# Who waits for GpSimd's two output stores: ScalarE in place of SyncE, in a mixture-of-experts MLP

## The chip, the cores and the metric

The kernel runs on one core of a Trainium2 chip. The metric is the device time of one execution in microseconds (us), the median of several runs. Beside it there is one profiled execution, whose trace is read below.

## The reference

Eight experts, each a two-layer perceptron on its own 256 tokens, in float32:

```python
n_experts, capacity, hidden, expert_hidden = 8, 256, 512, 2048
h = np.matmul(x, w1) + b1[:, np.newaxis, :]      # 8 x (256x512 @ 512x2048)
h = np.maximum(h, 0)
return (np.matmul(h, w2) + b2[:, np.newaxis, :]).astype(np.float32)   # 8 x (256x2048 @ 2048x512)
```

## The kernel before

The weights stream from memory, 4 MB for each of two matrices and each expert, and are cast to float16 on their way by the DMAs that GpSimd issues. TensorE works on one expert after the other: step `s` of its loop makes the hidden layer of expert `s` (`ph`, line 292), and the output layer of expert `s - LAG` (`po`, line 314), with `LAG = 3`. ScalarE applies bias and relu to the hidden layer (L226). VectorE transposes the tokens (L124). The output layer is taken out of PSUM by `evict` (L206): each of VectorE and ScalarE takes half of the tokens of every expert, VectorE the half that is finished last.

Nearly all of it is one section whose synchronisation is written by hand (`by_hand`, opened at L138 with SyncE, called SP here, as its synchronising engine). Inside it every engine has its own list of instructions, and semaphores that are waited for by hand hold them together. When the section ends, the engines meet at its exit, whose instructions carry the number L138 in the trace, and when the program ends, at a barrier that carries L353.

The results leave in two ways. Experts 0 to 3 and experts 4 and 5 are gathered in two tiles (`GROUPS = {0: 4, 4: 2}`), and `flush` stores each tile with one DMA in GpSimd's ring, 2 MB and 1 MB, as soon as both halves of the group's last expert are evicted. `load` (L88) issues them, and gives each a semaphore of its own, `landed["out0"]` and `landed["out4"]`, that counts to 16 when the data has landed. The last two experts (`HALVED`) are stored by SP itself, with `store` (L244), as soon as each is complete. Their landing is counted by `s_last`, and awaited behind the section.

SP's list hands out permission to TensorE: it waits for weights to land and for buffers to be free, and counts up `s_go` (`go`, L239 and L240). Its last steps are the waits for the final evictions (L268), the last store, and the wait for GpSimd's two stores (L271). ScalarE's list consists of the relu instructions and its half of the evictions; its last step is the eviction of its half of expert 7.

GpSimd's list holds all the loads of weights and then the two flushes; it does not wait for their landing.

Of the kernel before, what the change touches and what calls it, by code (L numbers as in the profile page):

```python
# [10 lines left out]
def kernel(  # L11
# [12 lines left out]
    nc = tc.nc  # L24
# [17 lines left out]
    GROUPS = {0: 4, 4: 2}  # L42
# [41 lines left out]
    landed = {}  # L84
# [19 lines left out]
    def transposes(e):  # L104
# [25 lines left out]
        out=b1_rows[:], in_=b1.rearrange("e (b i) -> (e b) i", b=nB)))  # L130
# [59 lines left out]
    for b in range(nB):  # L190
        turned = nc.vector.transpose(  # L191
            out=b1T[b * B : (b + 1) * B, nB - 1 - b : nB - 1 - b + nJ * B],
# [4 lines left out]
    def evict(e, tb):  # L197
        engine = nc.vector if tb else nc.scalar
        copy = nc.vector.tensor_copy if tb else nc.scalar.copy
        first, n = group_of.get(e, (e, 1))  # L200
        rows = P // n
        at = (e - first) * rows
        engine.wait_ge(s_po, nTB * e + tb + 1)
        for k in range(n):
            bank = (e % 2 * nTB + tb) * H
            last = copy(out=results[e][at : at + rows, k * nTB + tb, :],  # L206
                        in_=po[k * rows : (k + 1) * rows, bank : bank + H])
        last.then_inc(s_out[tb], 1)
# [8 lines left out]
    for s in range(E + LAG):  # L217
        if s < E:
            split = group_of.get(s, (s, 1))[1]
            if s > LAG:  # L220
                nc.scalar.wait_ge(s_po, nTB * (s - LAG))
            for j in range(nJ):
                mine = hT[:, s % (LAG + 1) * nJ * T : (s % (LAG + 1) + 1) * nJ * T]
                bias_at = j * B + s * nB + nB - 1
                nc.scalar.wait_ge(s_ph, nJ * s + j + 1)
                nc.scalar.activation(  # L226
                    out=mine.rearrange("p (tb j k i) -> p j tb k i", tb=nTB, j=nJ, k=split)[:, j],
                    in_=ph[:, j % NPH, 0:T].rearrange("p (tb i k) -> p tb k i", tb=nTB, k=split),
                    func=relu,
                    bias=b1T[:, bias_at : bias_at + 1],  # L230
                    scale=1.0,
                ).then_inc(s_credit, 1)
        if s >= LAG:
            evict(s - LAG, 0)

# [4 lines left out]
    def store(e, p0, p1, engine):  # L242
        dst = out[e].rearrange("(p r) h -> p r h", r=nTB)
        engine.dma_start(out=dst[p0:p1], in_=results[e][p0:p1]).then_inc(s_last, 16)  # L244
# [22 lines left out]
    for tb in range(nTB):  # L267
        nc.sync.wait_ge(s_out[tb], E)  # L268
    store(E - 1, 0, P, nc.sync)
    for first in GROUPS:  # L270
        nc.sync.wait_ge(landed[f"out{first}"], 16)  # L271


    nc.tensor.sem_inc(s_credit, NPH)
# [83 lines left out]
```

## Time and profile before

| what | us |
|---|---|
| median of 3 runs | 181.86 |
| lowest and highest | 181.73, 181.88 |
| profiled execution, its own time | 182.14 |
| its span, first to last instruction | 180.4 |

The span is what the trace covers; times in the trace are counted from its start. The engines are called PE (TensorE), DVE (VectorE), ACT (ScalarE), POOL (GpSimd) and SP (SyncE). A "q" behind the name means the engine's instruction queue: waits, drains, branches and DMA issues, which are not counted as busy. A row for a source line reads: engine and operation, how many, their durations in nanoseconds (least, median, greatest), and the start of the first and the last of them in us. A row of waits reads: who waited, for whom, total us, how often, longest us.

### The profile page before, as it was taken

Reading aid. Unit: us, or ns where it says so; the run is one execution under the profiler, and the core shown is the slowest. Engines: PE = TensorE matmul, PEld = TensorE weight load, DVE = VectorE, ACT = ScalarE, POOL = GpSimd, SP = SyncE. Lnnn points to the kernel's source line nnn. Section 1 sums busy time; section 2 is a strip of 40 time slices with the busy share of each in tenths; the row PEclk is TensorE's granted clock in tenths of the full one; section 3 lists DMA queues with packets and bytes.
Section 4 is the critical chain, followed back from the end, with each engine's and each line's share of the span. In section 5 each row is a group of like instructions: output and inputs, shape, how many; then the busy total and the mean of one; then the engine's idle time right before and its main releaser. Section 6 shows DMA issues by size and latency. Waiting matters only on the chain. (4 is left out here: it accounts for less than half of the span.)

```text
span 180.4 us, 2999 instructions
## 1 busy us (share of the span) xinstructions
PE 134.9 (75%) x784; PEld 92.5 (51%) x784; DVE 86.8 (48%) x124; ACT 75.6 (42%) x153; POOL 12.5 (7%) x27
## 2 busy tenths in 40 slices
PE   0004969868688970998978896889688979996960
PEld 0003869868688430794378544864388434442320
DVE  1989929585000399996099807990510020201010
ACT  3201777757588040492557352763188010110100
POOL 6000021020200010001010001000200011010000
PEclk9999999999999998599999999999999999999995
DMA  5998999999899999989999999999899999999994
GB/s 229 251 229 180 233 229 205 207 229 227 185 233 202 234 203 233 225 185 229 229 214 196 233 225 203 211 229 225 189 229 229 211 207 215 220 218 172 380 422 169
DMA packets 3826, 40.46 MB, mean 224 GB/s; under 512 B 448, under 2 KB 464, under 8 KB 1392
## 3 DMA queue, kind: packets, MB, share of 16 engines
q0 software_dynamic: 3200, 38.28, 96.2%
q1 hardware_dynamic: 576, 2.10, 2.9%
q10 hardware_dynamic: 48, 0.07, 0.1%
q14 instruction: 2, 0.02, 0.0%
HBM read 71.39 MB, written 4.19 MB: 419 GB/s over the span
## 5 line engine op out<-in xcount | busy, mean ns | idle before, releaser
L292 PE MATMUL ph<-xT,w_sb 128*128 x512 | 72.3, 302 | 33.1 <-PEq L277 30.1
L292 PEld LDWEIGHTS ph<-xT,w_sb 128*128 x512 | 66.7, 146 | 39.7 <-issue 31.0
L226 ACT ACTIVATE hT<-ph,b1T 128x256 f16<-128x256 f32 x128 | 60.2, 475 | 47.1 <-PE ph L292 43.6
L124 DVE STREAM_TRANSPOSE xT<-x 32x256 f16<-32x256 f16 (+1 forms) x64 | 52.8, 893 | 25.2 <-DMA x<-in_x_dram 22.1
L314 PE MATMUL po<-w_sb,hT 128*128 x256 | 58.1, 380 | 0.0
L314 PEld LDWEIGHTS po<-w_sb,hT 128*128 x256 | 24.4, 97 | 29.5 <-issue 4.0
L206 DVE COPY out<-po 32x512 f32<-32x512 f32 (+1 forms) x20 | 13.7, 687 | 42.6 <-PE po L314 42.4
L206 ACT COPY out<-po 32x512 f32<-32x512 f32 (+1 forms) x20 | 11.5, 577 | 28.7 <-PE po L314 28.5
L88 POOL DMA_DIRECT2D w_sb<-in_w_dram x18 | 9.7, 544 | 137.4 <-PE po L314 71.3
L121 DVE STREAM_TRANSPOSE xT<-x 32x256 f16<-32x256 f16 x32 | 14.0, 436 | 0.5
L309 PE MATMUL po<-b_sb,ones 1*128 x16 | 6.1, 383 | 6.2 <-issue 3.6
L206 DVE COPY x<-po 128x512 f32<-128x512 f32 x2 | 1.4, 692 | 15.3 <-PE po L314 15.3
L309 PEld LDWEIGHTS po<-b_sb,ones 1*128 1x128 f16 x16 | 1.4, 90 | 12.0 <-issue 12.0
L206 ACT COPY x<-po 128x512 f32<-128x512 f32 x2 | 1.2, 586 | 15.3 <-PE po L314 15.3
L191 DVE STREAM_TRANSPOSE b1T<-b_rows 32x512 f32<-32x512 f32 x4 | 4.1, 1026 | 0.5 <-issue 0.5
L135 ACT CAST x<-x 128x1024 f16<-128x1024 f32 x1 | 1.0, 1044 | 3.2 <-DMA x<-in_x_dram 3.2
L133 DVE CAST x<-x 128x1024 f16<-128x1024 f32 x1 | 0.7, 695 | 3.0 <-DMA x<-in_x_dram 3.0
L88 POOL DMA_DIRECT2D out_dram<-out x2 | 1.1, 538 | 9.2 <-DVE out L206 9.2
L128 ACT ACT_TABLE_LOAD x1 | 1.3, 1283 | 0.7 <-PEq L342 0.7
L88 POOL DMA_DIRECT2D x<-in_x_dram x2 | 1.1, 550 | 0.0
L127 DVE MEMSET ones<- 1x128 f16 x1 | 0.2, 165 | 0.9 <-PEq L342 0.9
L88 POOL DMA_DIRECT2D b_sb<-in_b_dram x1 | 0.5, 509 | 0.0
(5 smaller groups left out, 0.7 us busy)
## 6 DMA issues: line engine op xcount, KB each, us to landing
w_sb<-in_w_dram POOLq DMA_DIRECT2D x14, 2048.0 KB, 41.2
w_sb<-in_w_dram POOLq DMA_DIRECT2D x2, 1536.0 KB, 22.5
out_dram<-out POOLq DMA_DIRECT2D x1, 2048.0 KB, 25.3
x<-in_x_dram SPq DMA_DIRECT2D x2, 512.0 KB, 3.8
x<-in_x_dram POOLq DMA_DIRECT2D x1, 1024.0 KB, 34.6
w_sb<-in_w_dram POOLq DMA_DIRECT2D x2, 512.0 KB, 24.7
out_dram<-out POOLq DMA_DIRECT2D x1, 1024.0 KB, 18.5
out_dram<-x SPq DMA_DIRECT2D x2, 512.0 KB, 6.6
```

Source lines behind the costliest of these rows:

```text
L88: engine.dma_start(**kw).then_inc(landed[key], 16)
L121: last = nc.vector.transpose(out=dst[:, :, g, :, 0, :], in_=block[:, :, :, 0, :])
L124: last = nc.vector.transpose(out=dst[:, tb, g], in_=block[:, tb])
L128: tc.keep_in_program_order(nc.scalar.activation(out=warm[:], in_=ones1[:], func=relu))
L133: nc.vector.tensor_copy(out=x16[0][0][:], in_=x32[0][:])
L135: tc.keep_in_program_order(nc.scalar.copy(out=x16[1][0][:], in_=x32[1][:]))
L191: turned = nc.vector.transpose(out=b1T[b * B : (b + 1) * B, nB - 1 - b : nB - 1 - b + nJ * B], in_=b1_rows[:].rearrange("r (i j) -> r j i" ...
L206: last = copy(out=results[e][at : at + rows, k * nTB + tb, :], in_=po[k * rows : (k + 1) * rows, bank : bank + H])
L226: nc.scalar.activation(out=mine.rearrange("p (tb j k i) -> p j tb k i", tb=nTB, j=nJ, k=split)[:, j], in_=ph[:, j % NPH, 0:T].rearrange("p ...
L292: last = nc.tensor.matmul(ph[:, j % NPH, 0:T], w1_sb[:, bass.ds(w_from + (kc * M + j), P, nJ)], xT[:, bass.ds(x_at + kc * T, T)], start=(k ...
L309: nc.tensor.matmul(bank, ones1[:], b2_sb[:, bass.ds(s * H, H)], start=True, stop=False)
L314: last = nc.tensor.matmul(bank, hT[:, bass.ds(t * (nJ * P // H) + j * P, P)], w2_sb[:, bass.ds(w_at + j * H, H)], start=False, stop=(j == ...
```

## The change

Two wait instructions move. In SP's list they stood at the end, behind the last store. They now stand at the end of ScalarE's list, behind its last eviction. The semaphores, the values that are waited for, and all else are the same.

```diff
@@ ScalarE's list @@
         if s >= LAG:
             evict(s - LAG, 0)
+    for first in GROUPS:
+        nc.scalar.wait_ge(landed[f"out{first}"], 16)
@@ SP's list @@
     for tb in range(nTB):
         nc.sync.wait_ge(s_out[tb], E)
     store(E - 1, 0, P, nc.sync)
-    for first in GROUPS:
-        nc.sync.wait_ge(landed[f"out{first}"], 16)
```

## The prediction

> **What bounds the kernel now.** I read the page first, for its span, then the chain of waits, then the waits of SP's own queue, and last the lines behind the section's end, because everything that the change touches lies there.
>
> The page gives the span, and how long each store to the output takes from issue to landing. The large stores leave through GpSimd's ring (POOLq), two of 512 KB through SP's queue.
>
> ```profile
> span 180.4 us, 2999 instructions
> out_dram<-out POOLq DMA_DIRECT2D x1, 2048.0 KB, 25.3
> out_dram<-out POOLq DMA_DIRECT2D x1, 1024.0 KB, 18.5
> out_dram<-x SPq DMA_DIRECT2D x2, 512.0 KB, 6.6
> ```
>
> The chain that ended last closes with VectorE's eviction of the last half of the last expert:
>
> ```profile
> 174.20 0.02 issue
> 174.22 0.69 DVE x L206
> ```
>
> So the arithmetic is over at 174.22 + 0.69 = 174.9 us, and 180.4 - 174.9 = 5.5 us of the span come behind it. The chain does not say what fills them, since no computing engine is busy there. SP's waits from 174 us on say more:
>
> ```profile
> SPq L268 <- DVE x L206: 6.1, 1, 6.1
> SPq L271 <- DMA out_dram<-out: 2.0, 1, 2.0
> SPq L353 <- PEq L353: 1.5, 2, 1.1
> SPq L138 <- DMA out_dram<-x: 0.7, 1, 0.7
> ```
>
> In order: SP is released at 174.9 by that eviction, issues the last store, waits 2.0 us for the ring's stores (L271, the wait that the change moves), waits 0.7 us for its own two stores (L138), and then waits once more for 1.1 us at L353, the barrier at the end of the program. That last wait is the interesting one: both of SP's reasons to wait are gone by then. The releaser printed beside it is PE's sequencer; whether that is true is shown by the arrivals at the barrier. First the store and the moved wait, by source line:
>
> ```profile
> L244 SPq DMA_DIRECT2D out_dram<-x x2: 344/346/347, 165.9 to 175.0; - x2
> DMA to landing us min/median/max: 3.6/6.6/9.6
> L271 SPq EVENT_SEMAPHORE  x1: 17/17/17, 177.4 to 177.4; - x1
> ```
>
> The last store is issued at 175.0. Its landing is the 3.6 of the three, as 175.0 + 9.6 would lie beyond the span: 175.0 + 3.6 = 178.6. The ring's stores are through at 177.4. Next, the exit of the section (L138):
>
> ```profile
> L138 SPq EVENT_SEMAPHORE  x4: 17/22/735, 177.6 to 177.9; - x4
> L138 ACTq DRAIN  x1: 8/8/8, 177.6 to 177.6; - x1
> L138 POOLq NOP  x1: 13/13/13, 177.6 to 177.6; - x1
> L138 DVEq DRAIN  x1: 17/17/17, 177.6 to 177.6; - x1
> L138 PEldq DRAIN  x1: 8/8/8, 177.6 to 177.6; - x1
> ...
> L138 SPq NOP  x1: 13/13/13, 178.7 to 178.7; - x1
> ```
>
> All five engines leave the section together at 177.6, 0.2 us behind L271, though ScalarE, VectorE, TensorE and GpSimd had nothing left to do: they stood waiting for SP's signal. The 735 ns among SP's four is its wait for its own stores, over at 178.6. Last, the program's end between 177.65 and 179.68 us, and GpSimd's share of the rest:
>
> ```profile
> L353 SPq DRAIN  x2: 7/7/7, 178.7 to 178.8; - x2
> L353 ACTq DRAIN  x1: 8/8/8, 177.7 to 177.7; - x1
> L353 POOLq DRAIN  x1: 1929/1929/1929, 177.7 to 177.7; - x1
> L353 PEldq DRAIN  x1: 8/8/8, 177.7 to 177.7; - x1
> L353 DVEq DRAIN  x1: 10/10/10, 177.8 to 177.8; - x1
> ...
> L353 POOLq EVENT_SEMAPHORE  x4: 17/17/17, 179.7 to 180.3; - x4
> L353 POOLq DRAIN  x2: 45/68/90, 179.9 to 180.1; - x2
> ```
>
> These are the arrivals. TensorE, ScalarE and VectorE are there at 177.7 to 177.8, SP at 178.8. GpSimd starts its drain at 177.7 and needs 1.93 us for it: 177.7 + 1.93 = 179.6, and its barrier instruction follows at 179.7. So GpSimd, not PE, comes last, 0.9 us behind SP. What ends the program today is this chain: the ring's last landing (177.4), SP's signal (177.6), GpSimd's drain (to 179.6), the barrier (to 180.4).
>
> **The change part by part.** *Removed from SP:* two waits behind the last store, in front of the exit signal. SP issues the store from 175.0 to 175.35 either way. Without the waits it goes on to the signal, 0.2 us later by the distance of L271 to L138: about 175.55 in place of 177.6. No row shows a shorter or longer way; the 0.2 could be some tenths more while the transfers are running, which costs nothing, as shown below. SP's next steps stay where they are, since they wait for its own last store: 178.6, the two drains at 178.7 and 178.8.
>
> *GpSimd's drain, moved with the signal.* This is the whole gain. It starts 0.1 us behind the signal, at 175.65 instead of 177.7. Its length there is not shown, because the trace has no drain of GpSimd with a store of its ring in flight. The nearest rows are the 1929 ns above and, on the other side, the 45 and 90 ns of its two later drains. I take the 1929, as it is the only one that stands directly behind the ring's transfers: 175.65 + 1.93 = 177.6. The short end would give 175.7. If the drain also has to see the ring's last store land, and only adds a short end to that (45 to 90 ns), it is over at 177.4 + 0.1 = 177.5. All of these lie before SP's arrival at 178.8, so the uncertainty hides behind SP's wait for its last store. The cover is 178.8 - 177.6 = 1.2 us: the drain could take 3.1 us and cost nothing.
>
> *Added to ScalarE:* two waits behind its last copy.
>
> ```profile
> L206 ACT COPY x<-po x2: 586/586/586, 160.8 to 170.0; 128x512 f32<-128x512 f32 x2
> L88 SPq COMPARE_BRANCH  x1: 33/33/33, 177.4 to 177.4; - x1
> ```
>
> That copy ends at 170.0 + 0.59 = 170.6, and ScalarE does nothing from there to its exit drain at 177.6. Behind the waits are queued only this drain and the one of L353. Who waits for them: SP, which collects the exit marks of all engines before it turns to its own landing, and the barrier. The waits end at 177.4 as they did on SP; a wait instruction is 17 ns (L271) and the jump out of the section 33 ns; with the 0.2 us that SP needed, ScalarE's exit drain is at 177.6 as before, and SP's collecting is done 0.1 us later. It needs it by 178.6. The cover is about 0.9 us; without it, that is if the ring's store landed at 178.3 or later, the end would move with the landing. The signal itself needs nothing of ScalarE: in the stretch from 177.5 to 177.63 us L138 has one instruction, and it is SP's.
>
> ```profile
> L138 SPq EVENT_SEMAPHORE  x1: 17/17/17, 177.6 to 177.6; - x1
> ```
>
> All the others of L138, ScalarE's drain among them, stand behind it.
>
> *Not moved:* the issue of any transfer. No DMA is added, removed or put into another queue, and the two stores in question left GpSimd long before. VectorE and TensorE reach the barrier some 2 us earlier, for which nobody waits.
>
> *The sum.* The barrier now opens when SP arrives. GpSimd's barrier instruction moves from 179.7 to 178.8, where SP's drain is, and the 0.7 us from there to the end of the span stay (179.7 to 180.4). The gain is 179.7 - 178.8 = 0.9 us. The profiled execution took 182.14 us with its span of 180.4, so 1.7 us lie around it; 182.14 - 0.9 = 181.24. The median of the runs shown is 181.86, 0.28 below that execution, so I forecast 181.86 - 0.9 = 180.96 us. What is late next is SP's last store: 3.6 us from issue to landing, all of it on the path.
>
> **A rule against it.** The row for GpSimd is 1929 ns of drain. The Trainium skill, "VectorE: DVE Perf Modes", section "The DRAIN you can't avoid", says that the drains in front of and behind a kernel are a constant of about 12 ns on all five engines. The trace agrees for four engines (7 to 10 ns) and differs by far on GpSimd. By the rule SP would already be last today and the change would bring nothing; by the row it brings 0.9 us.
>
> **The rivals.** *The drain pays in full behind its ring's landing.* If the 1.93 us are work that can only begin when the ring is empty, it ends at 177.4 + 1.93 = 179.3, and the barrier instruction stands at 179.35 or 179.4: a gain of 0.35, 181.51 us. For it: the one drain shown began 0.3 us behind the landing, so its beginning could have been bound to it. Against it: a drain whose cost is a pass over what the ring has done can make most of that pass before the last landing. These are the ring's transfers, by groups of the page:
>
> ```profile
> L88 POOL DMA_DIRECT2D w_sb<-in_w_dram x18 | 9.7, 544 | 137.4 <-PE po L314 71.3
> L88 POOL DMA_DIRECT2D out_dram<-out x2 | 1.1, 538 | 9.2 <-DVE out L206 9.2
> L88 POOL DMA_DIRECT2D x<-in_x_dram x2 | 1.1, 550 | 0.0
> L88 POOL DMA_DIRECT2D b_sb<-in_b_dram x1 | 0.5, 509 | 0.0
> ```
>
> They are 18 + 2 + 2 + 1 = 23; spread over them, 1.93 us would be 0.08 us each, and only one is unfinished after 175.65.
>
> *The drain is a wait for every store, or the signal is not freed.* If the drain ended a fixed time behind the last landing of any queue (179.6 - 178.6 = 1.0 us), or if the section's exit still made SP wait for ScalarE ahead of the signal, the end would stay where it is: 181.86. For the first: 1.93 us is long for an instruction with nothing to compute, and the last store was in flight during it. Against: nothing lands at 179.6, and a wait for the landing would have ended at 178.6. Against the second: SP's signal stands ahead of ScalarE's drain.
>
> *Slower: the drain gets in the way of the last store.* Today it begins when the DMA engines are nearly idle; then it would run among full traffic, as the windows of 175.0 to 177.4 and of the time behind it show (the last two columns are the DMA share and GB/s):
>
> ```profile
> 175.00:177.40 2.40, 0.00 (x0) 0.00 (x0) 0.00 (x0) 0.00 (x0) 0.00 (x0) 0.75 0.97 405
> 177.40:180.40 3.00, 0.00 (x0) 0.00 (x0) 0.00 (x0) 0.00 (x0) 0.00 (x0) 0.50 0.13 53
> ```
>
> The last store's landing is the bound after the change, so every delay of it counts in full. If the drain held the engines for its whole length, the store would land at 178.6 + 1.93 = 180.5, and the end would be 1.93 - 0.9 = 1.0 us later than now: 182.9 us. It decides against the change from a delay of 0.9 us on. For it: the first of SP's stores took 9.6 us beside the ring's traffic. Against it: that was 3 MB of stores queued ahead, while a drain moves no bytes by any row, and today's drain already ran beside the last microsecond of that store without a mark on it.
>
> **How the numbers follow.** The forecast has 0.80, the drain in full behind the landing 0.07, no change 0.08 (0.06 by the landing, 0.02 by the exit), slower 0.05. A measurement of this kernel can tell about 0.2%, 0.36 us, from no change. The forecast's 0.9 us is 0.5% and clearly outside; the first rival's 0.35 us is on the border, and I give it half to each side: faster 0.84, same 0.11, slower 0.05. The range runs from 180.80 (the forecast, less the 0.15 us by which the three runs of before differ) to 181.55, just beyond the first rival, and so holds 0.87.
>
> **What would show it.** In the profile after: SP's L138 signal and GpSimd's L138 NOP near 175.6; GpSimd's long drain from about 175.7 with an end before 178.8; SP's last L353 wait down from 1.1 us to about 0.1; no L271-like wait on SP, and the 0.7 us wait for its own stores grown to about 3 us, less what ScalarE's exit mark takes of it. The span should be 179.5. A drain that ends at 179.3 makes the first rival right, one that ends at 179.6 the second; a last store that takes clearly more than 3.6 us makes the slower case right. I would be wrong altogether if GpSimd's NOP still stood at 177.6.

## The result, and the profile after

The kernel with the change took 181.10 us (median of 8 runs), the one before 181.89 us over all 8 of its runs. The medians differ by 0.79 us. Over the single runs the ratio is 0.9947, with a 95% interval of 0.9928 to 0.9965: a gain of 0.96 us (0.64 to 1.31). The forecast was 0.9 us.

The profiled execution took 181.10 us with a span of 179.3, against 180.4 before. Of the 1.1 us between the spans, 0.18 belong to an earlier start of the end: VectorE's last eviction began at 174.04 instead of 174.22. The rest, 0.9 us, lies behind that eviction. The end of the chain of waits, and then SP's waits from 173 us on, to be held against the four rows of before:

```profile
174.02 0.02 issue
174.04 0.69 DVE x L206
```

```profile
SPq L270 <- DVE x L206: 6.1, 1, 6.1
SPq L138 <- ACTq L138: 2.0, 1, 2.0
SPq L138 <- DMA out_dram<-x: 1.0, 1, 1.0
SPq L353 <- PEq L353: 0.6, 2, 0.4
```

The 2.0 us that SP stood at its own wait for GpSimd's stores are still there. It now spends them at the section's exit, waiting for ScalarE, which does the waiting. What has gone is the wait at the last barrier: 1.5 us in two waits before, 0.6 now. By source line, the last store, ScalarE's added wait, the exit (L138), and the end of the program up to 178.75 us:

```profile
L246 SPq DMA_DIRECT2D out_dram<-x x2: 344/346/348, 166.0 to 174.8; - x2
L236 ACTq EVENT_SEMAPHORE  x1: 17/17/17, 177.2 to 177.2; - x1
L138 SPq EVENT_SEMAPHORE  x4: 17/482/2019, 175.2 to 177.5; - x4
...
L138 POOLq NOP  x1: 13/13/13, 175.2 to 175.2; - x1
L138 DVEq DRAIN  x1: 17/17/17, 175.2 to 175.2; - x1
...
L138 ACTq DRAIN  x1: 8/8/8, 177.4 to 177.4; - x1
```

```profile
L353 SPq DRAIN  x2: 7/7/7, 178.6 to 178.6; - x2
L353 POOLq EVENT_SEMAPHORE  x2: 17/17/17, 178.7 to 178.7; - x2
L353 POOLq DRAIN  x1: 2875/2875/2875, 175.3 to 175.3; - x1
L353 PEldq DRAIN  x1: 8/8/8, 175.4 to 175.4; - x1
L353 DVEq DRAIN  x1: 10/10/10, 175.4 to 175.4; - x1
L353 ACTq DRAIN  x1: 8/8/8, 177.5 to 177.5; - x1
```

SP signals at 175.2, GpSimd leaves the section in the same moment, and its drain runs from 175.3 to 175.3 + 2.88 = 178.2. SP arrives at 178.6, and the barrier instruction follows at 178.7: SP, not GpSimd, is now last. But the drain has become 2.88 us long where it was 1.93. Of the cover of 1.2 us that the prediction counted on, 0.4 us are left. Why the drain grew is the question of most of the experiments.

### The profile page after: what moved, and what is told of

It reads as the page before. It is cut to its first block, busy times and chain, and to the rows that moved or that the text cites. A ratio compares the mean times of both kernels' runs of the same rounds, so it can differ in the third digit from the quotient of the medians.

```text
span 179.3 us, 2999 instructions
## 1 busy us (share of the span) xinstructions
PE 135.0 (75%) x784; PEld 92.5 (52%) x784; DVE 86.7 (48%) x124; ACT 75.7 (42%) x153; POOL 12.5 (7%) x27
```

## The experiments

Three theories were put against each other. Theory 1: the gain is the drain that starts earlier; at first with its 1.93 us, and from experiment 5 on with an end that follows the last landing in GpSimd's ring. Theory 2: the drain is a fixed piece of work that DMA traffic stretches. Theory 3: SP gains from having less to wait for, whatever the drain does.

**1. The change again.** No edit.

> The change itself once more, unaltered. All theories: 180.95 us, 0.9 below the kernel before, ratio 0.995. In the trace, GpSimd's long drain starts within 0.2 us of SP's exit signal (175.2 us). If its 2.9 us of the first profile are no accident, it ends 1.0 us behind the last landing of GpSimd's ring and about 0.4 us ahead of SP's arrival at the last barrier.

Measured: 180.99 us, ratio 0.9945 (0.9925 to 0.9965).

```profile
L236 ACTq EVENT_SEMAPHORE  x1: 17/17/17, 177.5 to 177.5; - x1
L353 POOLq DRAIN  x3: 45/90/2641, 175.8 to 179.3; - x3
```

The drain is 2641 ns here and 2875 ns above, but in both it ends the same time behind the landing of the ring's last store. From landing to end, by the nanoseconds of the trace, it is 177.451 to 178.433 here and 177.218 to 178.199 above: 0.982 and 0.981 us. Its end, not its length, is what repeats.

**2. The wait on GpSimd itself.**

```diff
+    for first in GROUPS:                 # behind GpSimd's flushes
+        nc.gpsimd.wait_ge(landed[f"out{first}"], 16)
-    for first in GROUPS:                 # ScalarE's list
-        nc.scalar.wait_ge(landed[f"out{first}"], 16)
```

> The two waits stand at the end of GpSimd's own list, behind its last store issue, so SP's signal is as early as in the change (175.2) but GpSimd reaches its drain only at about 177.3. Theory 1 (the gain is the drain that runs earlier): the drain takes its 1.93 us from 177.3, ends at about 179.25, after SP's arrival at 178.6; the time is 0.6 us above the change and 0.3 to 0.4 us below the kernel before: 181.5 us. Theory 2 (the drain is a fixed piece of work that traffic of the DMAs stretches): the same end, give or take 0.2 us. Theory 3 (the gain comes from SP having less to wait for, wherever the wait goes): as the change, 180.95 us.

Measured: 181.90 us, ratio to the kernel before 1.0011 (0.9990 to 1.0033).

```profile
L187 POOLq EVENT_SEMAPHORE  x1: 17/17/17, 177.4 to 177.4; - x1
L138 SPq EVENT_SEMAPHORE  x4: 17/22/2915, 175.4 to 175.7; - x4
L138 POOLq NOP  x1: 13/13/13, 177.7 to 177.7; - x1
L353 POOLq DRAIN  x3: 45/90/1929, 177.7 to 180.1; - x3
```

SP is as free as with the change, its signal comes at 175.4, and nothing is gained. That ends theory 3: the drain starts at 177.7 and takes 1929 ns, both as before. All theories had erred by 0.4 us in the start: between GpSimd's wait and its drain lie the same 0.3 us (177.4 to 177.7) that SP's way over the signal had cost.

**3. The wait on SP, behind its signal.** The two ring stores count on one semaphore, awaited where SP awaits its own stores. The lines of the wait:

```diff
-    landing = nc.sync.nop().wait_op(s_last, 16 * len(HALVED), "sem-ge")
+    for s_done, n in ((s_last, len(HALVED)), (s_ring, len(GROUPS))):
+        landing = nc.sync.nop().wait_op(s_done, 16 * n, "sem-ge")
```

> SP keeps the wait for GpSimd's two stores, but behind its exit signal: both stores count on one semaphore of their own, which is awaited where SP awaits its own two stores. Theories 1 and 2: what matters is the signal, which is early; 180.95 us as with the change, GpSimd's drain from 175.3, SP last at the barrier. Theory 3 (SP must be rid of the wait): no gain, 181.85 us.

Measured: 181.01 us, ratio 0.9950 (0.9932 to 0.9968), the gain of the change.

```profile
L140 SPq EVENT_SEMAPHORE  x4: 17/22/2851, 175.0 to 175.4; - x4
L140 POOLq NOP  x1: 13/13/13, 175.1 to 175.1; - x1
```

So ScalarE has no part in it. SP may keep the wait, as long as the signal goes out first. The drain took 2783 ns here, from 175.16 to 177.94, once more 0.98 us behind the ring's last landing (176.96).

**4. The signal later still.** SP awaits all stores, its own too, ahead of the signal. The edit is one to the kernel before, without the change:

```diff
     for first in GROUPS:
         nc.sync.wait_ge(landed[f"out{first}"], 16)
+    nc.sync.wait_ge(s_last, 16 * len(HALVED))
```

> The other way: SP awaits GpSimd's two stores and also its own two inside the section, ahead of the signal, so the signal comes at about 178.7 in place of 177.6 and nothing is in flight any more when GpSimd's drain starts. Theory 1: the drain takes 1.93 us whole, from 178.7 to 180.7; the time is 1.0 to 1.1 us above the kernel before, 182.9 us. Theory 2: with no traffic at all the drain is shorter than the 1.93 us, say 1.0 to 1.5 us, and the time 0.2 to 0.6 us above the kernel before, 182.1 to 182.5 us. Theory 3: as the kernel before, 181.9 us.

Measured: 183.30 us, ratio 1.0084 (1.0053 to 1.0114). The median is 0.4 us above what theory 1 expected; the interval holds its 1.0 us, and the profiled spans differ by 181.4 - 180.4 = 1.0.

```profile
L354 POOLq EVENT_SEMAPHORE  x4: 17/17/17, 180.7 to 181.3; - x4
L354 POOLq DRAIN  x3: 45/90/1929, 178.7 to 181.1; - x3
```

The drain takes 1929 ns with no store in flight, and it took 1929 ns in the kernel before and in experiment 2 with SP's last store in flight. So one store in flight does not stretch it, against theory 2. That store was little traffic, a DMA share of 0.14 from 177.7 to 178.6 us in the kernel before; experiments 6, 7 and 8 show the drain in more.

**5. The last store in the ring.** GpSimd issues the store of expert 7 as a third store of its ring, and ScalarE awaits that too. The lines that move the store:

```diff
+    for tb in range(nTB):                # behind GpSimd's flushes
+        nc.gpsimd.wait_ge(s_out[tb], E)
+    load(nc.gpsimd, f"out{E - 1}", in_=results[E - 1][:], ...
-    store(E - 1, 0, P, nc.sync)
```

> On the base of the change, GpSimd's ring also takes SP's last store (expert 7), so that the ring's last landing is the last of all, near 178.5 to 178.9 us, and ScalarE awaits it too. Theory 1, sharpened by the runs so far (the drain cannot end before 0.98 us behind the ring's last landing): the drain starts near 175.8 and ends at 179.5 to 179.9, behind SP's arrival; the time is 0.9 to 1.2 us above the change, about the kernel before or 0.2 us above it: 181.9 to 182.2 us. Rival (a drain in full traffic takes up to 2.9 us from its start, whatever lands): it ends by 178.7, SP remains last, 181.0 to 181.3 us.

Measured: 181.96 us, ratio 1.0003 (0.9985 to 1.0022): the gain is gone.

```profile
L240 ACTq EVENT_SEMAPHORE  x1: 38/38/38, 178.5 to 178.5; - x1
L356 POOLq EVENT_SEMAPHORE  x4: 17/17/17, 179.5 to 180.1; - x4
L356 POOLq DRAIN  x3: 45/96/4073, 175.4 to 179.9; - x3
L356 SPq DRAIN  x3: 7/7/7, 178.9 to 179.7; - x3
```

The drain now lasts 4073 ns, to 179.49, again 1.0 us behind the ring's last landing at 178.46, and GpSimd is last once more, 0.5 us behind SP. A store in this ring costs about 1 us after it has landed; the same store in SP's queue costs 0.2 us (landing 178.4, barrier 178.7 in the profile after).

**6. The stores out of the ring.** SP issues both large stores. The line that changes the queue; `flush` now also stands in SP's list:

```diff
-        load(nc.gpsimd, f"out{first}", in_=results[first][:],
+        load(nc.sync, f"out{first}", in_=results[first][:],
```

> On the base of the change, the two large stores leave through SP's queue in place of GpSimd's ring, each as soon as SP knows that its results are there; GpSimd's ring is then empty from about 170 us on, while SP's queue still moves data at full rate to the end. Theory 1: the drain takes exactly 1.93 us from its start, as its ring is empty. Rival (traffic): 2.6 to 2.9 us, as in the change. The total time is no matter here, since the stores now compete with the loads of weights: 181 to 186 us.

Measured, one run: 187.29 us, 1.3 us above the upper end of the expectation. The ring's loads of weights now land later (the last at 175.8 in place of 168.6).

```profile
L353 POOLq DRAIN  x3: 45/90/1766, 182.5 to 185.2; - x3
```

```profile
182.50:184.30 1.80, 0.00 (x0) 0.00 (x0) 0.00 (x0) 0.00 (x0) 0.00 (x0) 1.00 0.72 291
```

The second row is the stretch of the drain. Its DMA share, the last column but one, is 0.72: SP's last store was under way, though not at the full rate that was expected. The drain is not longer for it, so the rival falls. But it is not exactly the 1929 ns of theory 1 either, it is 1766. The ring has two transfers less, 21, and the drain is 163 ns shorter: 82 ns for each.

**7 and 8. Twenty more transfers in the ring**, of 512 bytes each, results unused, with the early signal (7, ScalarE awaits them) and with the late one (8, SP awaits them; base is the kernel before). The line that issues them:

```diff
+        nc.gpsimd.dma_start(out=spare[...], in_=b2[0:1, 0:256]...).then_inc(s_extra, 16)   # x20
```

> On the base of the change, 20 further tiny loads of 512 bytes are put into GpSimd's ring during the middle of the run, 43 transfers in place of 23, their results unused. If the drain passes over all the transfers of its ring, and that pass lies behind the last landing, the 0.98 us behind the ring's last landing become about 1.8 us. If that part is fixed, it stays 0.98 us. The time itself: up to 1 us above the change.

> The same 20 further loads, but with all landings awaited by SP ahead of its signal, so the drain starts with nothing in flight and shows its whole own length. If it passes over all transfers, 1.93 us become 43/23 of it, 3.6 us, or about 2.7 us if only the half ahead of or behind the landing grows. If it is fixed, 1.93 us. The time: 183 us, up to 1.7 us more if the drain grows.

Measured, one run each: 182.66 and 186.07 us, 0.6 and 1.4 us above the upper ends of the expectations. A part of this lies ahead of the end: VectorE's last eviction began 1.0 and 1.2 us later than in the change and in experiment 4 (175.06 and 175.22), and of each 0.2 us lies outside the span (2.0 where the change has 1.8). Why, no run shows. The drain of each, and the stretch in which it ran:

```profile
L363 POOLq DRAIN  x3: 51/96/3567, 176.3 to 180.4; - x3
```

```profile
176.30:178.00 1.70, 0.00 (x0) 0.00 (x0) 0.00 (x0) 0.00 (x0) 0.00 (x0) 1.00 0.99 410
```

```profile
L364 POOLq DRAIN  x3: 51/96/3567, 179.7 to 183.8; - x3
```

```profile
179.70:183.30 3.60, 0.00 (x0) 0.00 (x0) 0.00 (x0) 0.00 (x0) 0.00 (x0) 0.50 0.00 0
```

Both are 3567 ns, the 3.6 us of the pass over all transfers. In experiment 7 the DMA engines were full (0.99) for the drain's first 1.7 us, in experiment 8 they stood still (0.00): here theory 2 falls, for full traffic too. With 21, 23 and 43 transfers at 1766, 1929 and 3567 ns, each transfer costs 82 ns and 45 ns remain, about the length of the shortest drain behind (45 in the first two, 51 with 43). In experiment 7 the ring's last landing (178.0) came 1.6 us after the drain's start and did not lengthen it, where in the change 1.9 us did. So part of the pass can run ahead of the landing, and it is longer with more transfers.

**9. Half of the last store earlier**, as a try for something better than the change. The calls, on ScalarE and SP:

```diff
+    half_of_last(0, nc.scalar)           # ScalarE, behind its last eviction
-    store(E - 1, 0, P, nc.sync)
+    half_of_last(1, nc.sync)
```

> On the base of the change, the store of expert 7 is cut in two: ScalarE issues its half of the tokens when it has evicted it (near 171 us), SP only the other half at 174.8. It asks whether the last store, which ends the change's path, can be shortened. If it is bound by its issue (3.6 us from issue to landing for 512 KB), half of it lands up to 1 us earlier, and GpSimd's drain (178.2) then ends the path: 0.4 us below the change, 180.55 us. If the DMA engines are full to the end (their share is 1.0 up to 177.4 us in the change), the same bytes end at the same time: 180.9 to 181.1 us, and the rows of 2 KB instead of 4 KB may cost a little.

Measured: 181.21 us, ratio to the kernel before 0.9959 (0.9944 to 0.9973): no better than the change. The rows of the drain and of SP, and the stretches of time with the DMA share in the last column but one:

```profile
L357 POOLq DRAIN  x3: 45/90/3473, 175.2 to 179.1; - x3
L357 SPq DRAIN  x3: 7/7/7, 178.4 to 178.9; - x3
```

```profile
175.00:177.40 2.40, 0.00 (x0) 0.00 (x0) 0.00 (x0) 0.00 (x0) 0.00 (x0) 1.00 0.98 399
177.40:179.40 2.00, 0.00 (x0) 0.00 (x0) 0.00 (x0) 0.00 (x0) 0.00 (x0) 0.80 0.18 67
```

The engines are as full as before up to 177.4. SP's half lands 0.1 us earlier (178.3), but the early half pushed the ring's last store from 177.2 to 177.7, and the drain follows to 178.7, behind SP's 178.5. What is taken from one of the two ends goes to the other.

**10. Experiments 5 and 7 together**, 44 transfers and the last landing in the ring. The edit is that of both.

> Experiments 5 and 7 together: 44 transfers in GpSimd's ring, 20 of them tiny loads without use, and the ring's last landing as the last of all, about 3 us behind the drain's start. It asks which part of the drain grows with the transfers. If half of the 82 ns for each transfer lies ahead of the ring's last landing and half behind it, the drain ends 44 x 0.041 + 0.04 = 1.84 us behind the last landing. If the part behind the landing is fixed, it ends 1.0 us behind it, as with 23 and 24 transfers. The time: 1.0 to 1.9 us above the kernel before.

Measured, one run: 184.37 us, 2.5 us above the kernel before and 0.6 above the upper end; the 20 loads also delay what is ahead of the end. ScalarE's waits for the ring's last two stores, and the drain:

```profile
L250 ACTq EVENT_SEMAPHORE  x2: 17/28/38, 178.4 to 179.5; - x2
L366 POOLq DRAIN  x3: 51/102/4697, 176.7 to 181.8; - x3
```

The drain ends at 176.67 + 4.70 = 181.37, and the ring's last store had landed at 179.53: 1.84 us, as the halves give. So in these runs the drain ends 0.041 us for each transfer, and 0.04 more, behind the later of two moments: the ring's last landing, and 0.041 us for each transfer behind its own start. With 23 transfers this is 0.94 ahead and 0.98 behind, with 24 it is 1.02 behind (experiment 5), with 44 it is 1.84. Why it is halves, two passes over the ring or one of two steps, no run shows.

## Why the prediction was right

*The sum.* Gain 0.9 us forecast, 0.96 measured (0.64 to 1.31; 0.79 by the medians); time 180.96 forecast, 181.10 and 180.99 measured. Its core step, that the barrier instruction moves from where GpSimd's drain ends to where SP arrives, holds: 179.7 before, 178.7 after, 0.18 of it from the earlier start. Experiments 2 and 3 show what makes the gain: that GpSimd leaves the section early. In experiment 2 SP's signal was early too, but GpSimd stood at a wait of its own, and nothing was gained; in experiment 3 SP kept the wait behind its signal, and the gain was there.

*SP's signal* came at 175.2, not 175.55. Of the difference 0.18 us is the earlier start; for the rest, the 0.2 us between wait and signal did not follow the store's issue, which ended at 175.16. This changed nothing, as SP's own store was later, as forecast.

*The drain* is the step that was sized wrong. The prediction took 1.93 us from the start, an end at 177.6, and argued that a pass over the transfers leaves only the last one undone after the landing. The pass was right, 82 ns for each where 0.08 had been estimated, but half of the whole follows the last landing. The end was 178.2, 0.6 us later than forecast. The time came out all the same because of the cover behind SP's last store, which the prediction had put at 1.2 us: the end is still 0.4 us ahead of SP. With a third store in the ring (experiment 5) or 20 small loads (experiment 7, drain to 179.9, SP there at 179.4) it would not have been.

*ScalarE's wait* cost nothing: its exit drain stood at 177.4, 1.0 us ahead of SP's last landing, and SP's wait split into the 2.0 and 1.0 us that the prediction described.

*The rivals.* That the drain pays in full behind the landing was half true, 0.98 of 1.93 us. That it waits for every store fell in the first profile, where it ended 0.25 us before SP's last store landed (178.45). That SP's signal would still wait for ScalarE fell with the signal at 175.2, ahead of ScalarE's exit drain at 177.4. That the drain slows SP's last store fell with 3.6 us from issue to landing before and after. The rule that drains at the ends are about 12 ns on all engines (the Trainium skill, "VectorE: DVE Perf Modes", section "The DRAIN you can't avoid") speaks of drains that the runtime puts around a kernel. The drains here carry a line of the kernel (L353), and GpSimd's, behind its own DMAs, took 1766 to 4697 ns in these runs, so the rule could not be carried over to it.

## What to carry to other kernels

Behind the last computation, list when each engine arrives at the last barrier; the releaser printed beside a barrier wait can be a wrong one. If GpSimd has issued DMAs, its drain can take time for each of them (82 ns here, half of it behind the ring's last landing where that is late), so let it start early and keep the last landing out of its ring. A wait at the end is best placed where nothing hangs on it that comes last. Here that was on ScalarE, or on SP behind its signal, as SP's own last store landed 1.2 us later than the ring's; on GpSimd nothing was gained.

## What the runs showed of the hardware that was not expected

GpSimd's drain at the program's end took 45 ns + 82 ns for each DMA that GpSimd had issued in the whole program, where its ring's last landing did not hold it up. Twenty more of 512 bytes added 1638 ns, and two less, of 2 MB and 1 MB, took 163 ns away, so the size did not matter. That the DMAs that had landed more than 150 us before count as well follows from the 45 ns that remain when all are counted, about the length of the shortest later drain; no run varied the early ones alone. The drain was the same to the nanosecond (1929) in three kernels. With transfers in flight it grew up to 4697 ns by the rule above. TensorE's, VectorE's and ScalarE's drains at the same place took 7 to 10 ns.
